# Two-layer MLA and S5 backbone: powers on VectorE, table loads tied to gates and units, other places for tables and gates

## The chip, the core and the metric

The kernel runs on one core of a Trainium2 chip. The metric is the device time of one execution in microseconds (us), as the median of several runs. PE is the matrix engine (TensorE), PEld its weight loads, DVE the vector engine, ACT the scalar engine, POOL is GpSimd, and SP the engine whose queue issues most DMAs. Each engine works through its own instructions in the order in which they stand in its queue, and so does each queue of DMA issues.

## The reference

The input is a latent stream of 512 tokens and a context of 256 tokens, 1024 wide. Layer 0 is multi-head latent attention with 16 heads and a SiLU gate, layer 1 a bidirectional S5 state-space layer with GLU. Both are modulated by a condition and end in a residual with LayerNorm. Cut to what matters here:

```python
# layer 0, attention over the low-rank keys (per head), then gate and projection
p = softmax((concat[q_pos @ keys_lat, q_free @ keys_ctx]) * scale)
o = p[:s] @ ckv_l + p[s:] @ ckv_c
y = ((o @ w_uv) * silu(gate)) @ w_out
x = layernorm(ALPHA * x + gt * y)
# layer 1, S5 in each direction, chunks of the sequence carried by a state
lam_bar = exp(lam * dt);  b_bar = ((lam_bar - 1) / lam) * bmat
powers  = exp(lam * dt * arange(1, S5_CHUNK + 1))
xs = scan(lam_bar, u @ b_bar) + powers * h;  y = real(xs @ cmat)
```

The S5 recurrence does not need the input to prepare its weights: powers of `lam_bar`, and from them tables that turn blocks of 8 tokens into states, states into outputs, and a short convolution kernel. The kernel makes these weights beside the work of layer 0 and leaves them in DRAM for layer 1.

## The kernel before

All tokens (768, latent and context) lie in the free dimension, channels in the 128 partitions. Products in fp32 are made of three matmuls of fp32r halves: `split` (L64) lets ACT copy the high half (`whi`) and DVE subtract it for the low half (`wlo`), and `mm3` (L80) issues hi by hi, hi by lo, lo by hi. `schedule_with_timeline_sim=True` (L1493) means that the framework puts the instructions of each engine in an order of its own, found with a simulated timeline; the order of the source is a priority, and a tile that is asked for takes a buffer as soon as its last user has released it.

Layer 0 runs through these stages.

- **Start** (L524 to L626). In four quarters `mod_part(q)` loads modulation weights into 24 staging tiles. They come in a cycle from pool `gv` (4 tiles `G`), pool `gm` (7 tiles `M`) and the two `pair` tiles. `h_make` makes the modulated input `hh`, `hl` (8 tiles of each). Meanwhile `s5_params` (L155) computes on DVE the step sizes, exponentials, cosines and the first power `lbr, lbi`, and then on POOL (`cmul`, six instructions of 128x128) the powers `pk` 0 to 7, their products with the coefficient in `cps`, the copies into `pw`, and four squarings `lt`, which go by five SP DMAs to `lamd`. Its tiles are the later `Qh0, Qh1, Ql0, Ql1, Vh, Vl, K1, K2, Ch, Cl` of attention: arena and `lt` lie in `Qh0, Qh1, Ql0`, `cps` in `K1, K2, Ch`.
- **Projections and gates** (L653 to L753). First come the four projections to `ckv`, `qd`, `kr`. Then `s5_coefs` (L295) turns `cps` with 16 PE transposes and stores it to `pind`; only after it do `K1, K2, Ch` come free for the keys. `gate(m)` for m = 0 to 15 (48 matmuls each) writes a gate tile. The first `KEPT = 4` stay in `G` tiles, the other twelve go through two `Gs` tiles to DRAM (`Gd`). Between the gates run 24 steps of the remaining modulation weights (`mod_more`, each a DMA of 768 or 512 KB into a `pair` tile), and `tables(n)`, which makes `S5IN = 20` of the `NCH = 32` chunks of state-out weights.
- **A chunk** (`s5_chunk`, L318): SP loads `cb`; POOL makes six products of 128x512 into `wo` and four smaller ones into `bk`; PE multiplies `bk` by `wo`; ACT and DVE take the result to `ks`; SP stores `wo` to `wod` and `ks` in eight DMAs to `kd`.
- **Attention** (L754 to L886): 16 heads of 5 units each, 80 units. Unit i takes `score(i + 2)`, transposes, values, `up_values` (multiplies by the gate, L840) and `softmax(i + 2)`. `prep(h + 1)` makes the next head's queries; in it the low halves `ul` (128x128, each head) and `wlo` (128x512, every second head) are subtracted on POOL (`split(..., pool)`, L460 and L500). `gate_back` reloads the twelve gates from DRAM. The other 12 chunks are made at the rate of 5 in 8 units. After unit `LAST = 19`, in two of three units, `win_early` makes the 32 pieces of state-in weights.
- **A piece of state-in weight** (`win_early`, L389): SP stores the piece made last (`wid`, L394), SP loads the next one's two tables of 512 KB (`pt` from `pind`, L375, into one of two `wo` tiles; `bt` from `Bc`, L376, into one of two halves of `btp`), and POOL makes the piece loaded before with six instructions of 128x512 (`win_make`, L378).
- **Out projection** (L889 to L998): 2 halves of 16 heads, 18 matmuls of 128x512 per head; ACT and DVE split `wraw` into `whi`, `wlo` in 7 buffers ahead. POOL has nothing to do here. Residual, norm and layer 1 follow; layer 1 reads `wid`, `wod`, `kd`, `lamd`.

## Time and profile before

| | us |
|---|---|
| median of 3 runs (1795.07 to 1800.5) | 1798.24 |
| the profiled execution | 1801.8 |
| its span, first to last instruction | 1800.0 |
| PE busy in the span | 1569.4 (87%) |
| DVE, ACT, POOL busy | 955.2, 731.0, 660.4 |
| mean granted clock of TensorE | 0.937 of full speed |

The page gives busy times for the whole span and for 40 equal slices. Busy PE is modelled, and at a lower granted clock the same matmul counts as busy for longer, so busy time is read together with the granted clock. The stages of layer 0 are read with a table of busy times in chosen stretches, the waits of each engine in such a stretch, and the instructions in order of time. A wait is put down to the instruction that came last.

### The profile page before, as it was taken

To read this page: it belongs to the slowest core of one execution; us is meant where nothing else is said; L and a number is where in the kernel's file an instruction comes from. 1 tells how busy PE (TensorE), PEld (TensorE's weight loads), DVE (VectorE), ACT (ScalarE), POOL (GpSimd) and SP (SyncE) were. 2 spreads that over 40 slices of the span, in tenths; PEclk is the share of its full clock that TensorE was granted. 3 is DMA by queue.
4 is the path that set the end of the run, shared out by engine and by line. 5 is a ranking of instruction groups with operands and counts; after the bars stand their busy time and mean duration, and the time that the engine had idled before them with its cause. 6 is when DMAs were issued, how large, how long until landed. Compare 5 with 4: busy or idle time off the path is not lost.

```text
span 1800.0 us, 26887 instructions
## 1 busy us (share of the span) xinstructions
PE 1569.4 (87%) x9870; PEld 1311.4 (73%) x9870; DVE 955.2 (53%) x2478; ACT 731.0 (41%) x1253; POOL 660.4 (37%) x705
## 2 busy tenths in 40 slices
PE   7547799988898789689999999889649999999997
PEld 4425568877787778678879999767437888888876
DVE  7252233476675567473472688868643333333336
ACT  2221122455564456272245666655444222222220
POOL 2999789899687777740000000000000000000022
PEclk9769899999998899889999999989769999999999
DMA  9226775532555555544327555599583333333342
GB/s 333 73 67 204 250 233 166 190 103 93 154 174 172 164 167 160 167 131 153 100 98 243 194 207 188 134 296 247 120 178 115 116 117 106 106 106 109 126 163 70
DMA packets 139340, 283.11 MB, mean 157 GB/s; under 512 B 38300, under 2 KB 70088, under 8 KB 139208
## 3 DMA queue, kind: packets, MB, share of 16 engines
q1 hardware_dynamic: 120904, 272.78, 49.5%
q10 hardware_dynamic: 18240, 8.59, 1.8%
q8 instruction: 78, 1.28, 0.3%
q14 instruction: 54, 0.44, 0.1%
q0 software_dynamic: 64, 0.03, 0.0%
HBM read 224.10 MB, written 56.97 MB: 156 GB/s over the span
## 4 chain that ended last, share of the span: by engine, by line
PE 49%; DMA 19%; POOL 17%; DVE 6%; issue 4%; ACT 3%; SPq 2%; ACTq 0%; POOLq 0%; DVEq 0%
PE mm L81 14%; PE mm L83 13%; PE mm L82 13%; DMA wo<-pind 5%; PE mm L1122 3%; DMA wid<-wo 3%; DMA toe<-kd 2%; DMA wraw<-in_wout_dram 1%; POOL wo L341 1%; POOL wo L338 1%; POOL wt L340 1%; POOL bk L352 1%; POOL wt L337 1%; DMA gd<-gg 1%; DMA pair<-in_w_mod_dram 1%
## 5 line engine op out<-in xcount | busy, mean ns | idle before, releaser
L65 DVE TENSOR_TENSOR wlo<-wraw,whi 128x1024 fp32r<-128x1024 f32 (+1 forms) x155 | 183.3, 1184 | 352.4 <-ACT whi L65 351.2
L1361 POOL TENSOR_TENSOR x<-x,row_g 128x1024 f32<-128x1024 f32 x4 | 11.4, 2852 | 968.1 <-DMA x<-x1d 968.1
L65 ACT CAST whi<-wraw 128x1024 fp32r<-128x1024 f32 (+1 forms) x155 | 149.5, 965 | 412.7 <-PE mm L82 278.2
L81 PE MATMUL mm<-st,whi 128*128 128x512 f32 x512 | 204.7, 400 | 7.4 <-ACT st L76 7.3
L83 PE MATMUL mm<-st,wlo 128*128 128x512 f32 x512 | 202.7, 396 | 0.0
L82 PE MATMUL mm<-st,whi 128*128 128x512 f32 x512 | 201.2, 393 | 0.5 <-DVE st L77 0.5
L81 PE MATMUL mm<-h,whi 128*128 128x512 f32 (+1 forms) x384 | 140.0, 365 | 12.3 <-DVE gg L1207 12.2
L82 PE MATMUL mm<-h,whi 128*128 128x512 f32 (+1 forms) x384 | 137.8, 359 | 0.8 <-DVE h L1067 0.8
L83 PE MATMUL mm<-h,wlo 128*128 128x512 f32 (+1 forms) x384 | 137.5, 359 | 0.0
L81 PEld LDWEIGHTS mm<-st,whi 128*128 128x128 f32 x512 | 97.5, 190 | 29.3 <-ACT st L76 8.7
L82 PEld LDWEIGHTS mm<-st,whi 128*128 128x128 f32 x512 | 97.3, 190 | 22.9 <-DVE st L77 1.5
L83 PEld LDWEIGHTS mm<-st,wlo 128*128 128x128 f32 x512 | 97.3, 190 | 22.6
L81 PE MATMUL mm<-hh,whi 128*128 128x512 f32 (+1 forms) x320 | 111.2, 358 | 2.9 <-DVE hh L589 2.9
L82 PE MATMUL mm<-hl,whi 128*128 128x512 f32 (+1 forms) x320 | 109.8, 346 | 0.0
L83 PE MATMUL mm<-hh,wlo 128*128 128x512 f32 (+1 forms) x320 | 108.7, 343 | 0.4 <-DVE wlo L65 0.3
L81 PEld LDWEIGHTS mm<-h,whi 128*128 128x128 f32 x384 | 73.6, 192 | 24.5 <-DVE gg L1207 13.3
L65 DVE TENSOR_TENSOR ptl<-tr,pth 128x384 fp32r<-128x384 f32 (+1 forms) x160 | 79.0, 523 | 17.1 <-ACT pth L65 16.3
L798 ACT ACTIVATE p<-sc,mx 128x768 f32<-128x768 f32 (+1 forms) x96 | 73.6, 767 | 32.2 <-DVE mx L797 32.0
L65 ACT CAST pth<-tr 128x384 fp32r<-128x384 f32 (+1 forms) x160 | 68.7, 462 | 41.9 <-PE tr L822 41.3
L797 DVE TENSOR_REDUCE mx<-sc 128x1 f32<-128x768 f32 (+1 forms) x96 | 73.6, 771 | 17.9 <-PE sc L787 16.7
L82 PEld LDWEIGHTS mm<-h,whi 128*128 128x128 f32 x384 | 73.7, 192 | 11.1 <-DVE h L1067 1.1
L83 PEld LDWEIGHTS mm<-h,wlo 128*128 128x128 f32 x384 | 73.5, 192 | 10.7
(371 smaller groups left out, 4188.3 us busy)
## 6 DMA issues: line engine op xcount, KB each, us to landing
wraw<-in_wglu_dram SPq DMA_DIRECT2D x64, 512.0 KB
wraw<-in_win_dram SPq DMA_DIRECT2D x52, 512.0 KB
wod<-wo SPq DMA_DIRECT2D x32, 512.0 KB
wo<-pind SPq DMA_DIRECT2D x32, 512.0 KB
pw<-in_Bc_dram SPq DMA_DIRECT2D x32, 512.0 KB
wid<-wo SPq DMA_DIRECT2D x32, 512.0 KB
pt<-wid SPq DMA_DIRECT2D x32, 512.0 KB
wo<-wod SPq DMA_DIRECT2D x32, 512.0 KB
```

What stands on the lines that cost most here:

```text
L65: return act.copy(hi, src).ins, (eng or dve).tensor_tensor(lo, src, f(hi), op=ALU.subtract).ins
L81: pe.matmul(ps, lh, rh, start=first, stop=False)
L82: pe.matmul(ps, lh, rl, start=False, stop=False)
L83: pe.matmul(ps, ll, rh, start=False, stop=last)
L337: pool.tensor_tensor(t2, ci, pi, op=ALU.mult)
L338: pool.tensor_tensor(wr, t1, t2, op=ALU.subtract)
L340: pool.tensor_tensor(t2, ci, pr, op=ALU.mult)
L341: pool.tensor_tensor(wi, t1, t2, op=ALU.add)
L352: pool.tensor_tensor(bk[rows, :, :, 16 * d:16 * d + 16], b1[rows], b2[rows], op=ALU.add)
L797: dve.reduce_max(mx[:, 1:2], s, axis=AX.X, negate=True)
L798: act.activation(p[:, a:b], s, AF.Exp, bias=mx[:, 1:2], scale=1.0, accum_out=mx[:, 2:3])
L1122: pe.matmul(o[:, r, 96 * q:96 * (q + 1)], wi[:, q, r, :], us[m][:, 4 * (c % 2) + q, :], start=True, stop=True)
```

## The change

1. **Powers on VectorE.** The chain of powers `pk` (8 `cmul`), the squarings `lt` (4), the first product `clr, cli` and five negations run on DVE. POOL keeps the eight products `cps` and the copies into `pw`. All eight `pk` have places of their own (`K1, K2, Ch`), `cps` lies in three `G` tiles. `s5_params` is a generator that is taken up again in the quarters of the start. The five stores to `lamd` are issued by ACT.
2. **Last gates kept.** Gates 12 to 15 stay in `G`, gates 0 to 11 go to DRAM and back (the first `AHEAD = 3` are asked for before attention, then one per head). `s5_coefs` runs after gate 1. The staging tiles of the start are the 16 tiles of `hh`, `hl`, then 7 `M` and one `pair`, so each of the 24 loads has its own.
3. **Table loads tied.** Before a load of `cb` (three buffers now) DVE copies one column of the gate just made, or of a softmax tile `p` of the next unit, into it; the load waits for that copy. The same is done for `bt`.
4. **`ul` and the rope `wlo` on DVE**, by the default of `split`.
5. **17 chunks** in the gates instead of 20; the other 15 in attention at 4 in 7 units, up to unit 26.
6. **State-in weights.** `pt` goes through three places: a tile `ext` that holds `cci` and the two `bk` before, and the two `wo`. They are made in 5 of 8 units after unit 26, and 24 of 32 there. The last eight are made in the out projection (`win_c`), in a pool of three `pt`, three `bt`, with their DMAs issued by ACT; the pool `w` of layer 1's weights opens after it closes.

```diff
-    KEPT = 4
+    KEPT, AHEAD = 4, 3
-    GR, NCH, S5IN = 128, 32, 20
+    GR, NCH, S5IN, WIN = 128, 32, 17, 24
...
-        cmul(clr, cli, cr, ci, lbr, lbi, t1, t2)
-        cps = [slots(6) for _ in range(3)]
+        cmul(clr, cli, cr, ci, lbr, lbi, t1, t2, dve)
+        u1, u2 = T1[:, 1, :], T1[:, 2, :]
+        cps, pk = [[slots(6, t) for _ in range(3)] for t in (take2, take)]
...
         for k in range(8):
+            p, q = pk[k], lt[0] if k == 7 else pk[k + 1]
+            cmul(q[:, 0, :], q[:, 1, :], p[:, 0, :], p[:, 1, :], lbr, lbi, t1, t2, dve)
+            cmul(cps[k][:, 0, :], cps[k][:, 1, :], p[:, 0, :], p[:, 1, :], clr, cli, u1, u2)
             pool.tensor_copy(pw[0:64, :, k, :], p[0:64])
             pool.tensor_copy(pw[64:128, :, 7 - k, :], p[64:128])
-            cmul(cps[k][:, 0, :], cps[k][:, 1, :], p[:, 0, :], p[:, 1, :], clr, cli, t1, t2)
-            q = lt[0] if k == 7 else pk[(k + 1) % 3]
-            cmul(q[:, 0, :], q[:, 1, :], p[:, 0, :], p[:, 1, :], lbr, lbi, t1, t2)
-            p = q
+            if k % 3 == 2:
+                yield cps
...
-            sp.dma_start(out=lamd[:, l], in_=lt[l])
+            act.dma_start(out=lamd[:, l], in_=lt[l])
...
         def load(c):
-            cbs[c] = work.tile([P, 4, 2, 32], F32, name="cb", bufs=2)
+            cbs[c] = work.tile([P, 4, 2, 32], F32, name="cb", bufs=3)
+            dve.tensor_copy(cbs[c][:, 0, 0, 0:1], after)
             sp.dma_start(out=cbs[c], in_=I["CB"][:, 4 * c:4 * c + 4])
...
-                split(*st["w"], raw, pool)
+                split(*st["w"], raw)
...
-                split(*st["u"], wa[:, 384:512], pool)
+                split(*st["u"], wa[:, 384:512])
...
-            wtile = itertools.cycle(["G"] * KEPT + ["M"] * 7 + ["pair"] * 2)
+            wtile = iter(["hh", "hl"] * KC + ["M"] * 7 + ["pair"])
...
-            s5_coefs(cps, mm, t512)
...
-                G.append(gv.tile([P, T], F32, name="G") if m < KEPT else gsp.tile([P, T], F32, name="Gs"))
+                G.append(gv.tile([P, T], F32, name="G") if m >= HEADS - KEPT else gsp.tile([P, T], F32, name="Gs"))
...
-                tables(3 if m == 0 else 1 + (m in (5, 10)))
+                if m == 1:
+                    s5_coefs(cps, mm, t512)
+                tables(1 + (m == 0), m)
...
-            LAST = 8 * (NCH - S5IN) // 5
+            LAST = 7 * (NCH - S5IN) // 4
...
-                    gate_back(h + KEPT)
+                    gate_back(h + AHEAD)
...
-                if LAST < i < len(units) - 1 and i % 3 != 0:
-                    win_early(lambda: (work.tile([P, 4, 2, P], F32, name="wo", bufs=2), btp[:, len(early) % 2]),
+                    pts = itertools.cycle([(s5c, "ext", [P, 9 * GR], 1)] + [(work, "wo", [P, 4, 2, P], 2)] * 2)
+                if i > LAST and 5 * i // 8 > 5 * (i - 1) // 8:
+                    def tabs():
+                        where, name, shape, bufs = next(pts)
+                        pt = where.tile(shape, F32, name=name, bufs=bufs)
...
+                        bt = btp[:, len(early) % 2]
+                        dve.tensor_copy(bt[:, 0, 0, 0:1], un[i + 1]["p"][:, 0:1])
+                        return pt, bt
+                    win_early(tabs, lambda: [work.tile([P, 4, P], F32, name=f"wt{k}", bufs=1) for k in (1, 2)],
+                              len(early) > NCH - WIN)
...
+    def win_c(more=True):
+        win_early(lambda: [wcp.tile([P, 4, 2, P], F32, name=n, bufs=3) for n in ("pt", "bt")],
+                  lambda: [wcp.tile([P, 4, P], F32, name=f"t{i}") for i in range(2)], more, act)
...
         if h == 7:
             gvs.close()
+            wces, (wcp,) = pools(dict(name="winc", bufs=2, side="right"))
         for tt in range(NT):
             out_mm(o[tt], tt, h, 0)
+        if h >= 7:
+            win_c()
...
-    assert not (early or loaded or stores)
+    while early or loaded or stores:
+        win_c()
+    wces.close()
```

## Rows read from the trace of the kernel before

**Rows 1.** The page's slices of 45 us: busy tenths of PE and POOL.

```profile
PE   7547799988898789689999999889649999999997
POOL 2999789899687777740000000000000000000022
```

**Rows 2.** Busy us (instructions) by stretch: PE, PEld, DVE, ACT, POOL; clock, DMA share, GB/s.

```profile
55.00:73.00 18.00, 17.33 (x90) 14.52 (x89) 6.73 (x7) 8.31 (x16) 16.69 (x29) 0.92 0.32 98
73.00:116.00 43.00, 13.92 (x43) 8.72 (x44) 13.02 (x14) 9.73 (x23) 40.14 (x70) 0.60 0.19 52
116.00:204.00 88.00, 57.36 (x487) 39.62 (x489) 33.66 (x49) 15.69 (x28) 84.01 (x102) 0.81 0.58 188
204.00:273.00 69.00, 64.16 (x606) 49.23 (x599) 21.27 (x34) 15.87 (x33) 52.47 (x59) 0.95 0.74 243
...
340.00:455.00 115.00, 104.95 (x1010) 90.76 (x1009) 76.93 (x162) 65.98 (x159) 108.38 (x126) 0.99 0.38 128
455.00:797.00 342.00, 282.22 (x1819) 253.13 (x1818) 216.83 (x444) 184.38 (x434) 256.84 (x208) 0.91 0.57 165
```

**Rows 3.** What PE waited for, 0 to 330 us: total us, times, longest.

```profile
PE modps L103 <- DMA pair<-in_w_mod_dram: 24.6, 8, 6.9
PE mm L300 <- POOL Ch L238: 12.9, 2, 6.8
PE mm L300 <- POOL K L238: 11.8, 3, 6.2
```

**Rows 4.** POOL in order of time: start us, us, line.

```profile
38.54 1.39 POOL L238 TENSOR_TENSOR Vh<-Ql,Vh 128x128 f32<-128x128 f32 x1
...
79.22 0.74 POOL L281 COPY pw<-Ql 64x256 f32<-64x256 f32 x1
...
81.66 0.45 POOL L238 TENSOR_TENSOR K<-Ql,Vh 128x128 f32<-128x128 f32 x1
...
86.60 0.39 POOL L281 COPY pw<-Vh 64x256 f32<-64x256 f32 x1
```

**Rows 5.** DVE in order of time, start and gates, to the first softmax reduction.

```profile
37.05 0.28 DVE L264 TENSOR_TENSOR Vl<-Qh,Vh 128x128 f32<-128x128 f32 x1
...
38.40 1.22 DVE L65 TENSOR_TENSOR wlo<-wraw,whi 128x1024 fp32r<-128x1024 f32 x1
...
116.52 0.69 DVE L689 SCALAR_TENSOR_TENSOR G<-G,mm 128x512 f32<-128x512 f32 x1 [0.50 <-ACT G L688]
...
204.19 0.69 DVE L689 SCALAR_TENSOR_TENSOR Gs<-Gs,mm 128x512 f32<-128x512 f32 x1 [8.66 <-ACT Gs L688]
...
273.07 0.69 DVE L689 SCALAR_TENSOR_TENSOR Gs<-Gs,mm 128x512 f32<-128x512 f32 x1
...
340.70 0.96 DVE L797 TENSOR_REDUCE mx<-sc 128x1 f32<-128x768 f32 x1 [2.12 <-PE sc L787]
```

**Rows 6.** What PE waited for, 460 to 800 us.

```profile
PE mm L83 <- POOL ul L65: 37.4, 5, 9.8
PE tr L822 <- DVE ptl L65: 12.6, 2, 12.4
```

**Rows 7.** What the SP queue waited for, 455 to 790 us.

```profile
SPq L394 <- POOL wo L385: 153.0, 31, 7.8
SPq L375 <- DMA wid<-wo: 79.3, 30, 6.1
```

**Rows 8.** DVE's products with the gate, two heads apart, and the last one.

```profile
589.73 0.41 DVE L840 TENSOR_TENSOR G<-mm,G 128x256 f32<-128x256 f32 x1
...
647.65 0.42 DVE L840 TENSOR_TENSOR G<-mm,G 128x256 f32<-128x256 f32 x1
...
794.77 0.42 DVE L840 TENSOR_TENSOR G<-mm,G 128x256 f32<-128x256 f32 x1 [0.38 <-PE mm L83]
```

**Rows 9.** A table load on the chain that ended last: start us, us.

```profile
585.84 8.22 DMA wo<-pind
```

**Rows 10.** ACT in the out projection, in order of time.

```profile
851.28 0.62 ACT L65 CAST whi<-wraw 128x512 fp32r<-128x512 f32 x1 [3.46 <-PE mm L83]
```

67 lines of the change are left out of this document (36 added, 31 removed).

## Prediction, made before the changed kernel was run

> **What bounds the kernel now.** The page's slices come first: PE is near full only from the ninth slice on, and dips again from the twelfth to the nineteenth, and just there POOL is at 7 to 9 tenths; after the eighteenth slice POOL is idle and PE full [rows 1]. So layer 0 is where PE loses time, and POOL is the suspect. The table of stretches makes that a list [rows 2]. From 73 to 116 us PE works 13.9 of 43 us at a granted clock of 0.60 while POOL works 40.1; from 116 to 204 it is 57.4 of 88 at 0.81, POOL 84.0. From 455 to 797 it is 282 of 342 at 0.91, POOL 257. A busy POOL proves nothing, so the third view is what PE waited for. At the start it is the transposes of `cps` (L300, 24.7 us in 5 waits) and the modulation weights (24.6 us in 8) [rows 3]. In attention it is `ul`, 37.4 us in 5 waits [rows 6]: a subtraction of half a microsecond that stands in POOL's queue behind six long products which themselves wait for a table. What these products wait for is seen from SP: the load of `pt` waits 79.3 us in 30 times for the store of the piece before, since that store frees its buffer [rows 7]. From 797 us on the change touches only the out projection.
>
> I make the sum from three marks: the first gate's product at 116.5 us, the first softmax reduction at 340.7 us [rows 5], and attention's last product with the gate at 794.8 us [rows 8].
>
> **Powers, coefficients and first gates.** A round of the chain on POOL took 7.38 us, from one copy into `pw` to the next (79.22 to 86.60), for 12 products and 2 copies, so 0.53 us each [rows 4]. Eight rounds with 6 products and 2 copies are 8 x 8 x 0.53 = 34 us; DVE has the coefficients at 37 us [rows 5], so POOL ends the rounds near 74 us and the chunks can follow; the squarings are gone from its queue (24 products, 13 us, beside the 8 x 6 powers, 25 us). DVE gains 54 + 24 products of 0.28 us [rows 5], at most 22 us, and 7 smaller ones. They run beside the loads of the start and between 55 and 73 us, where DVE works 6.7 of 18 us [rows 2]; if that cover fails they delay the last `hh`, 0 to 5 us, and I take 0. ACT's five stores cost it about 2 us in the same stretch (busy 8.3 of 18). The transposes of `cps` no longer stand ahead of `rms` and the first gate. With the 24.7 us of waits gone, and `K1` free near 74 us, the first gate's product comes at about 90 us instead of 116.5: 26.5 us earlier. Bounds are 84 (POOL free earlier than PE) and 100 (the keys still wait for `pw` copies).
>
> The trace shows POOL slowed beside DVE: a 128x128 product took 1.39 us at 38.5 us, where DVE began a 1.22 us subtraction at 38.4, and 0.45 us at 81.7 [rows 4, 5]. The Trainium skill (SBUF — State Buffer, "SBUF: two separate sides") says that DVE with two SBUF inputs and GpSimd exclude each other from a shared port pair for a whole instruction. By it the 78 moved products could push POOL's rounds out by up to 22 us, an estimate, to 96 us; by the row alone they end at 74. The first chunk's table waits for gate 0 anyway, so the sum would change by some 5 us.
>
> **Gates.** From gate 4's product to gate 9's there are 68.9 us [rows 5], 13.8 us per gate, with three modulation loads in each and the DMA at 0.74 share [rows 2]. From gate 9's to the first softmax are 67.6 us [rows 5]. After, POOL has 17 chunks instead of 20; at 84 us of 88 it was the pace from 116 to 204, at 52.5 of 69 it no longer was. So I take 13.8 us for each of gates 0 to 8: 90 + 9 x 13.8 + 67.6 = 282 us, against 340.7: **59 us less**. The low bound is 11.5 us per gate (between 13.8 and the 10 us of gates 9 to 15), which with the rest gives 84 + 104 + 67.6 = 256 and a gain of 85; the high bound is 16 us (four gates more are stored in the stretch where DMA is busiest), 100 + 144 + 67.6 = 312, a gain of 29. The tied table loads add a wait: DVE's copy into `cb` waits until POOL is through with the chunk three before, and behind it on DVE stand the gate's product (L689) and the weights' low halves, for which PE waits; on SP the load waits for the copy, and behind it stand the next gate's weights, the modulation loads and the stores of `Gs`. A chunk takes POOL less than 10 us and a gate 10 to 14, so I cost it at nothing; without that cover it is the difference per gate. The 12 gates stored and reloaded are as many as before, and the staging tiles change nothing as long as the start is bound by the loads themselves.
>
> **Attention.** Three paces follow each other. Up to unit 26 there are 15 chunks. In 340 to 455 us POOL was busy 108.4 us [rows 2] with 12 of them and 5 us of `ul` and `wlo`: 8.6 us each, 9.2 with gaps, so 138 us (the `ul` and `wlo`, now on DVE, cost it 0.3 to 0.7 us per head where it works 217 of 342 us; hidden). Then 24 pieces of state-in weights. POOL's 256.8 us in 455 to 797 hold 32 pieces and 11 us of `ul` and `wlo`: 7.7 us each. Before, each took the 342 - 10 us of the stretch over 32, 10.4 us, that is 7.7 plus the 2.6 us that SP waited for the store (79.3 over 30) [rows 7]. A third place takes that store out of the loop. A load takes 8.2 us [rows 9], about the time of a piece, so I take 7.7 + 0.6 = 8.3 us, 200 us for 24. Last come 15 units without POOL. Two heads took 57.9 us [rows 8] with about 8.6 us of waiting for `ul` (the mean of the five waits is 7.5, the largest 9.8 [rows 6]) and, by the clock of 0.91, some 2.5 us of half speed: 47 us for ten units, 4.7 each, 71 us. With 5 us for the last two units' lag: 138 + 200 + 71 + 5 = 414 us against 454: **40 us less**. `ul`'s 37.4 us and the 12.6 us at the end (a weight load behind the last pieces on SP [rows 6]) are inside it, not added. PE's own pace would give 80 x 4.7 + 5 = 381, 73 us less; the loop of 10.4 us kept gives 138 + 250 + 71 + 5 = 464, 10 us more. Here the new wait is DVE's copy into `bt`: it waits for POOL's piece two before, and behind it stand the reductions, the low halves of `p` and the products with the gate, so PE.
>
> **Out projection.** Eight pieces of 7.7 us, 62 us of POOL that had nothing to do there. ACT now stands still where a store waits for POOL, up to 7.7 us, with `whi` casts and the six copies of the half's end behind it. ACT was waiting for PE to free a buffer (3.46 us each time [rows 10]), seven tiles ahead, so casts are hidden; a copy that is caught costs PE directly. I take 2 us, bounds 0 and 10. Layer 1's weights load later, but before their use.
>
> **Sum.** 1801.8 - 59 - 40 + 2 = 1704.8 us for a profiled execution. The median before is 3.6 us below the profiled one, so I say 1701 us.
>
> **Rivals.**
> (a) POOL slips off the path altogether: gains of 80 and 73 us, out projection at 0, 1798 - 153 = 1645 us. For it speaks that PE needs POOL in attention only for a chunk's 16 small matmuls; against it that DVE's copies tie PE to POOL again, two pieces back.
> (b) The ties keep the old paces: 16 us per gate with the first at 92 us, 304 us and 37 us less; pieces at 10.4 us, 10 us more; out projection 8 us more: 1798 - 19 = 1779 us. SP's queue, where all these loads stand in one line, speaks for it.
> (c) Slower: the copy into `bt`, the load and the piece run one after the other because the copy comes behind the piece that POOL is working on. Then a piece costs 7.7 + 8.2 us, 16 us with handovers, 24 are 384 us instead of 200, and attention takes 598 us; with the other terms 1701 + 184 = 1885 us. It decides from about 12.3 us per piece, where the gains of 97 us are used up. Against it: there are two `bt` halves, and the load for one can run beside the piece of the other.
> (d) The change does not do what it says: the framework's order puts the chain of powers on DVE so late, or the transposes again so early, that the first gate stays at 116 us, and pieces keep their 10.4 us. Then only the chunks fewer and the tail move, 1785 to 1800 us.
>
> **How the numbers follow.** The forecast has a chance of 0.52, (a) 0.17, (b) 0.17, (c) 0.08, (d) 0.06. The forecast's own range is 1665 to 1740. Eight in ten have to take in (b) and nearly (a): 1648 to 1782 us. A measurement of this kernel tells about 0.3% (5.4 us) from no change; that band belongs to (d) mainly, so same has 0.04, slower 0.08, faster 0.88.
>
> **What would show it.** After: no wait of L300 for POOL's products, gate 0's product near 90 us, the first softmax reduction near 280; in attention no wait of PE for `ul`, pieces 8 to 9 us apart on POOL, attention some 414 us; POOL busy some 60 us in the out projection with PE still full. The prediction is wrong if DVE is seen idle before its copies into `cb` or `bt` until POOL ends (b, c), if PE waits for modulation weights for more than the 24.6 us of before, or if ACT's copies at the half's end stand behind a store.

## The result, and the profile after

The changed kernel took 1826.1 us in the median, the kernel before 1799.4 us in the same session: a ratio of 1.0138, with an interval of 1.0112 to 1.0164. The profiled execution of the changed kernel took 1826.06 us, with a span of 1823.9 us. The forecast was 1701 us. It was wrong, in sign too. One execution below that was kept as a trace, that of no_bt_tie, took over 1.5% longer than the fastest of its kernel; it is left out of that run's median and ratio, and its stretches are not compared.

All line numbers of this part are those of the changed kernel, where the product with the gate is L695, the first softmax reduction L807, attention's product with the gate L850, the copy into `cb` L324 and the one into `bt` L901. (Where an edit adds or removes a line, the numbers of its run are off by one or two.)

The marks come first: VectorE in order of time, as in [rows 5, 8].

```profile
99.20 0.68 DVE L695 SCALAR_TENSOR_TENSOR Gs<-Gs,mm 128x512 f32<-128x512 f32 x1
...
260.98 0.69 DVE L695 SCALAR_TENSOR_TENSOR Gs<-Gs,mm 128x512 f32<-128x512 f32 x1
...
334.19 0.96 DVE L807 TENSOR_REDUCE mx<-sc 128x1 f32<-128x768 f32 x1 [2.12 <-PE sc L797]
...
786.29 0.42 DVE L850 TENSOR_TENSOR G<-mm,G 128x256 f32<-128x256 f32 x1 [0.38 <-PE mm L83]
```

They split the change in the profiled spans, 1823.9 - 1800.0 = +23.9 us, into three terms:

| stretch | before | after | change | forecast |
|---|---|---|---|---|
| start to first softmax | 340.7 | 334.2 | -6.5 | -59 |
| first softmax to last product with the gate | 454.1 | 452.1 | -2.0 | -40 |
| from there to the end | 1005.2 | 1037.6 | +32.4 | +2 |

So two gains stayed out and a loss came where almost none was expected. The table of stretches answers [rows 2]: busy us with instruction counts in brackets for PE, PEld, DVE, ACT and POOL, then the granted clock, the DMA share and GB/s. The last two lines are the first 90 us of the output projection.

```profile
99.00:204.00 105.00, 77.23 (x621) 55.06 (x625) 41.00 (x68) 24.66 (x52) 68.46 (x70) 0.87 0.66 208
204.00:261.00 57.00, 47.81 (x397) 37.45 (x387) 14.46 (x30) 10.63 (x22) 35.45 (x40) 0.88 0.64 206
334.00:455.00 121.00, 101.33 (x904) 87.90 (x902) 76.27 (x170) 63.51 (x153) 94.94 (x110) 0.95 0.32 110
455.00:786.00 331.00, 284.89 (x2004) 251.00 (x2005) 230.53 (x495) 184.29 (x438) 221.73 (x184) 0.96 0.46 142
786.00:846.00 60.00, 56.43 (x243) 44.84 (x242) 25.80 (x31) 19.18 (x29) 22.20 (x18) 1.00 0.50 143
846.00:876.00 30.00, 10.88 (x47) 8.67 (x46) 6.96 (x9) 5.96 (x11) 19.58 (x15) 0.73 0.67 184
```

The last line is the most striking: PE works 10.9 of 30 us. In the same place before (855 to 885 us) it worked all 30:

```profile
855.00:885.00 30.00, 30.00 (x131) 24.42 (x130) 15.56 (x25) 8.13 (x14) 0.00 (x0) 1.00 0.43 132
```

In the stretches above, POOL is no longer the busy engine: it had 84.0 of 88 us in 116 to 204 before [rows 2], now 68.5 of 105. It waits.

**Gates.** What POOL waited for between 60 and 345 us (us in total, times, longest), and POOL's first chunk in order of time:

```profile
POOL wt L339 <- DMA cb<-in_CB_dram: 86.1, 12, 23.8
```

```profile
103.64 1.10 POOL L339 TENSOR_TENSOR wt<-cb,pw 128x512 f32<-128x512 f32 x1 [23.77 <-DMA cb<-in_CB_dram]
```

POOL had done its last product for the coefficients at 79.9 us and stood until 103.6, since the table load is tied to gate 0. Over the gates it stood 86.1 us for such tables.

**Attention.** DVE, then PE, in order of time around 540 us (`bt` lies in a tile that is named `pw`):

```profile
532.71 0.56 DVE L65 TENSOR_TENSOR ptl<-tr,pth 128x384 fp32r<-128x384 f32 x1
548.34 0.15 DVE L901 COPY pw<-p 128x1 f32<-128x1 f32 x1 [15.07 <-POOL wo L388]
548.41 0.55 DVE L65 TENSOR_TENSOR ptl<-tr,pth 128x384 fp32r<-128x384 f32 x1
```

```profile
536.07 0.49 PE L832 MATMUL tr<-ident,p 128*128 128x128 f32 x3
549.01 0.90 PE L832 MATMUL tr<-ident,p 128*128 128x128 f32 x3 [12.45 <-DVE ptl L65]
```

This is the tie at work. The copy writes one column of the `bt` half that POOL is still reading, so DVE stands 15.07 us until POOL's last instruction (L388) on that piece. The low half `ptl` behind it in DVE's queue comes late, and PE stands 12.45 us for it. The wait that PE had for `ul` (37.4 us [rows 6]) is gone, and this one and its like are in its place.

**Output projection.** A stretch of the chain that ended last (start us, us, what), and ACT in order of time:

```profile
799.57 3.36 DMA wraw<-in_wout_dram
...
836.76 7.16 DMA wraw<-in_wout_dram
...
847.86 9.21 DMA wraw<-in_wout_dram
```

```profile
869.98 0.62 ACT L65 CAST whi<-wraw 128x512 fp32r<-128x512 f32 x1 [2.92 <-DMA wraw<-in_wout_dram]
870.06 0.32 ACTq L397 DMA_DIRECT2D wid<-pt  x1
870.41 0.61 ACTq L379 DMA_DIRECT2D bt<-in_Bc_dram  x1
...
873.76 0.62 ACT L65 CAST whi<-wraw 128x512 fp32r<-128x512 f32 x1 [3.16 <-POOL t L384]
874.28 2.04 ACT L994 COPY acc<-mm 128x512 f32<-128x512 f32 x4
```

A 256 KB tile of output weights took 3.4 us at 799.6 us, before ACT issued the first load of a late piece (803.1 us); beside these loads it takes 7 to 9 us, and two are under way at most. ACT's six copies of the finished accumulators stand in its queue behind the casts of those tiles and behind the pieces' issues; they come 88.0 us after the last product with the gate, 61.3 us before the change. PE waits 19.1 us for them, and the granted clock of the stretch is 0.73.

```profile
PE mm L81 <- ACT acc L994: 19.1, 1, 19.1
```

How much of the +32.4 us belongs to the projection itself shows the last mean and variance of the norm at its end, before and after the change:

```profile
932.30 0.20 DVE L906 BATCH_NORM_AGGREGATE bnmv<-bnst 128x2 f32<-128x12 f32 x1
```

```profile
958.11 0.20 DVE L924 BATCH_NORM_AGGREGATE bnmv<-bnst 128x2 f32<-128x12 f32 x1
```

It comes 137.5 us after the last product with the gate before the change and 171.8 us after it, 34.3 us later. From there to the end it is 867.7 and 865.8 us. So the loss lies in the projection, and the new order of layer 1's loads, which could have been behind it, shows none. Below, this mark is called "the norm".

### The profile page after: what moved, and what is told of

Its sections match the earlier page's. It is cut to its first block, busy times and chain, and to the rows that moved or that the text cites. A ratio compares the mean times of both kernels' runs of the same rounds, so it can differ in the third digit from the quotient of the medians.

```text
span 1823.9 us, 27020 instructions
## 1 busy us (share of the span) xinstructions
PE 1585.2 (87%) x9870; PEld 1318.2 (72%) x9870; DVE 1006.3 (55%) x2643; ACT 729.9 (40%) x1253; POOL 606.5 (33%) x596
## 4 chain that ended last, share of the span: by engine, by line
PE 38%; DMA 15%; DVE 8%; POOL 4%; ACT 4%; issue 2%; SPq 0%; ACTq 0%; POOLq 0%; DVEq 0%
PE mm L81 11%; PE mm L82 11%; PE mm L83 11%; DMA wraw<-in_wout_dram 4%; PE mm L1148 3%; DMA pw<-in_Bc_dram 2%; DMA toe<-kd 2%; DVE wlo L65 2%; DMA wo<-wod 1%; DMA wraw<-in_win_dram 1%; ACT whi L65 1%; DMA gd<-gg 1%; DMA bt<-in_Bc_dram 1%; PE mm L1284 1%; POOL wt L384 1%
## 5 line engine op out<-in xcount | busy, mean ns | idle before, releaser
L81 PE MATMUL mm<-h,whi 128*128 128x512 f32 (+1 forms) x384 | 141.0, 368 | 11.9 <-DVE gg L1233 11.7
L83 PE MATMUL mm<-hh,wlo 128*128 128x512 f32 (+1 forms) x320 | 113.1, 358 | 3.5 <-DVE wlo L65 3.5
L82 PE MATMUL mm<-hl,whi 128*128 128x512 f32 (+1 forms) x320 | 114.6, 360 | 0.0
L81 PE MATMUL mm<-whi,vh 128*128 128x512 f32 x186 | 72.0, 408 | 25.6 <-ACT acc L994 19.1
L832 PE MATMUL tr<-ident,p 128*128 128x128 f32 x448 | 68.1, 276 | 23.2 <-DVE ptl L65 23.1
```

What stands on the lines that cost most here:

```text
L81: pe.matmul(ps, lh, rh, start=first, stop=False)
L82: pe.matmul(ps, lh, rl, start=False, stop=False)
L83: pe.matmul(ps, ll, rh, start=False, stop=last)
L832: pe.transpose(tp[:, n, :], p[:, j * P:(j + 1) * P], ident)
```

## The experiments

| run | edit, against the changed kernel | median us | ratio to before, interval |
|---|---|---|---|
| the change | | 1826.1 | 1.0138 (1.0112 to 1.0164) |
| all_in_attention | all 32 pieces in attention | 1830.5 | 1.0159 (1.0133 to 1.0185) |
| win_on_sp | late pieces' transfers on SP | 1824.2 | 1.0122 (1.0073 to 1.0171) |
| wraw4 | four places for output weights | 1819.1 | 1.0095 (1.0064 to 1.0126) |
| powers_pool | powers on POOL again | 1826.2 | 1.0139 (1.0097 to 1.0181) |
| no_gate_ties | no ties in the gates | 1815.2 | 1.0068 (1.0038 to 1.0098) |
| no_bt_tie | no ties for `bt` | 1802.6 | 1.0012 (0.9983 to 1.0041) |
| no_unit_ties | no ties in attention | 1774.4 | 0.9847 (0.9824 to 0.9870) |
| no_ties | no ties at all | 1767.9 | 0.9809 (0.9782 to 0.9836) |
| untied_late | no_unit_ties, pieces later in the source | 1768.7 | 0.9822 (0.9783 to 0.9862) |
| untied_28 | no_unit_ties, 28 pieces in attention | 1769.3 | 0.9813 (0.9782 to 0.9843) |
| untied_28_late | untied_late and untied_28 together | 1781.0 | 0.9869 (0.9821 to 0.9918) |
| chunks12 | no_unit_ties, 12 chunks in the gates | 1794.6 | 0.9955 (0.9927 to 0.9982) |
| nt_after | no_ties, pieces behind the copies | 1777.7 | 0.9879 (0.9857 to 0.9902) |
| nt_pool | no_ties, pieces' transfers on POOL | 1771.7 | 0.9836 (0.9785 to 0.9886) |
| nt_pool28 | nt_pool_wraw4, 28 pieces in attention | 1768.1 | 0.9811 (0.9763 to 0.9859) |
| nt_sp_wraw4 | no_ties, SP, four places | 1764.7 | 0.9803 (0.9744 to 0.9861) |
| nt_pool_wraw4 | no_ties, POOL, four places | 1757.2 | 0.9741 (0.9691 to 0.9791) |
| splits_only | the kernel before, with `ul` and `wlo` on DVE | 1815.5 | 1.0069 (1.0049 to 1.0089) |

The kernel before took 1799.4 to 1803.2 us beside these runs, so runs are compared by their ratios. Stretches are read from one profiled execution per run. The runs show how far such a reading can be trusted: attention with no ties in it and 24 pieces was 400.0, 400.1, 400.7, 403.6, 405.7, 407.5 and 408.4 us in seven of them, and the stretch after it, with the change's own output projection, 1030.9 to 1043.4 us in six (the change, powers_pool, no_gate_ties, no_unit_ties, no_ties, chunks12). A difference under 8 us in the first or under 13 us in the second means nothing here. Most of the latter's scatter lies behind the norm (860 to 871 us over all runs); up to the norm the same six took 169.2 to 174.7 us.

### The ties

```diff
 # no_unit_ties: attention; no_gate_ties: the same in the gates; no_ties: both
-                    chunk(work, mm, n_s5 - 1, NCH - 1, un[i + 1]["p"][:, 0:1])
+                    chunk(work, mm, n_s5 - 1, NCH - 1, None)
...
-                        dve.tensor_copy(bt[:, 0, 0, 0:1], un[i + 1]["p"][:, 0:1])
```

> The changed kernel without DVE's one-column copies into cb and bt in attention; the loads follow when their buffers are free. Theory: those copies hold DVE behind POOL (32.8 + 6.1 us for bt's places, 9.5 for cb), and with it reductions and low halves for PE, which waits 23.1 us for the transposes' input: attention from the first softmax to the last product with the gate falls from 452 to 415-440 us and the whole by 12-37 us. Rival: POOL itself is the pace of the pieces (SP waits 89.8 us for the store that frees a place, POOL 31.5 for bt): DVE no longer waits for POOL, but PE waits for something else, and attention stays at 447-457 us, the whole at 1820-1832.

Measured: 1774.4 us, 52 less than the change; attention 408.4 us. The theory held, and by more than it had given. Its rival fell: POOL's pieces did not hold attention at its old pace. What PE waited for in attention, first of the changed kernel, then without the ties (us, times, longest):

```profile
PE tr L832 <- DVE ptl L65: 23.1, 9, 12.4
```

```profile
PE mm L509 <- DMA wmod<-in_absw_dram: 8.9, 3, 3.6
...
PE tr L833 <- DVE ptl L65: 1.0, 3, 0.5
```

The wait for `ptl` falls from 23.1 to 1.0 us. The rest of the 44 us by which attention got shorter is not one wait of PE: the first chunk of attention began at 352.8 us where it began at 334 without the ties, and PE's mean clock in the whole execution went from 0.942 to 0.947.

```profile
352.82 1.23 POOL L339 TENSOR_TENSOR wt<-cb,pw 128x512 f32<-128x512 f32 x1 [20.77 <-DVE mx L809]
```

Here POOL stands 20.8 us for a table whose load was tied to a unit that PE had not reached. To tell the two kinds of tie apart:

> The changed kernel without the copy into bt that holds back a piece's second table; the copies into cb stay, in attention too. Without both kinds attention took 408.4 us instead of 452.1 and the whole 1774 instead of 1826. Theory A (the bt copies do it: DVE stood behind POOL 32.8 + 6.1 us for them, with the reductions and low halves behind): attention 410-420 us, the whole 1776-1790. Theory B (the cb copies do it: they stop the first chunk of attention for 20.8 us and the chunks at 447-467 us, so the pieces start at 518 us instead of 495): attention 425-440, the whole 1795-1815. If both halves of the loss are alike, 425-435 us.

Measured: 1802.6 us, inside theory B's range for the whole. By the ratios (1.0138 with both kinds, 1.0012, 0.9847 with neither) the `bt` copies carry some 23 us and the `cb` copies some 30. With intervals of 0.2 to 0.3% either way the two aren't told apart, and no run took the `cb` copies away alone. So a load that is held back costs in two ways: the engine that holds it stands (15.07 us before `bt`), and the consumer's work starts late (the first piece at 518 us with both kinds, at 495 without).

> The changed kernel without DVE's one-column copy that holds a chunk's table load back until its gate is there; everything else is kept. Theory: the ties starve POOL (86.1 us of waits for cb, 23.8 the longest, between 60 and 345 us), and PE's small matmuls of a chunk wait for POOL some 30 us in all. Without them POOL starts the chunks at 80 us, the waits for cb fall under 30 us, the first softmax comes at 300-320 us instead of 334.2, and the whole falls by 14-34 us to 1792-1812. Rival: the gates are paced by the loads of the modulation weights (PE waits 15.8 us for pairs) and by the DMA engines; then POOL is earlier but the first softmax stays at 330-336 and the whole at 1820-1830. A second rival: loads of tables that run ahead push the modulation loads back, first softmax 340 or later, 1832 us or more.

Measured: 1815.2 us, first softmax at 326.1 us. POOL's first chunk came at 57 us, but gate 0 moved back from 99.2 to 108.5 and gate 9 came forward only from 261.0 to 257.4. The theory had the sign, but its least gain was 14 us and 11 came; its rival (330 to 336 us for the softmax) fell too. Over the runs with 17 chunks the first softmax came at 329.7 to 335.1 us with these ties (nine) and at 325.0 to 330.8 without (seven), 5 us apart in the mean. So in the gates the ties cost some 5 to 11 us, not the 86.1 us that POOL stood.

> The changed kernel without any copy that ties a table load, in the gates or in attention. The two edits alone gave 1815.2 and 1774.4 us, against 1826.1. Theory (they act in different stretches and add): 11 us less than without the unit ties alone, 1758-1768 us, first softmax at 322-328, attention 404-412. Rival (the earlier chunks only give POOL an earlier start that attention doesn't need): first softmax 322-328 but attention 412-420, the whole 1768-1778.

Measured: 1767.9 us; first softmax at 325.0, attention 400.7, and 1038.4 us from there to the end. The two edits add, as the theory had it.

### The start and the gates

```diff
 # powers_pool: the products of the chain on POOL again (two more such lines: clr, cli and lt)
-            cmul(q[:, 0, :], q[:, 1, :], p[:, 0, :], p[:, 1, :], lbr, lbi, t1, t2, dve)
+            cmul(q[:, 0, :], q[:, 1, :], p[:, 0, :], p[:, 1, :], lbr, lbi, t1, t2)
```

> The changed kernel with the powers, the squarings and the first product of the coefficients on POOL again, in the new places and the new order; the ties stay. Theory (the products of DVE cost 0.50-0.55 us beside POOL's and hold the h tiles: the last cast of h at 61-69 us, before 54-57; DVE is through at 80 us): with them on POOL the start is 5-10 us shorter on DVE, but POOL ends its rounds at about 100-110 us instead of 79; as the first table comes at 103.6 us anyway, the first gate's product moves by -8 to +3 us from 99.2, the first softmax stays within 326-340 us, the whole within 1815-1832. Rival (POOL's early end is what brought gate 0 forward from 116.5): gate 0 back at 110-117, first softmax 345-352, the whole 1836-1845.

Measured: 1826.2 us, no change. Gate 0, gate 9 and the first softmax of this run, on DVE:

```profile
86.48 0.67 DVE L695 SCALAR_TENSOR_TENSOR Gs<-Gs,mm 128x512 f32<-128x512 f32 x1
...
258.04 0.69 DVE L695 SCALAR_TENSOR_TENSOR Gs<-Gs,mm 128x512 f32<-128x512 f32 x1
...
332.41 0.96 DVE L807 TENSOR_REDUCE mx<-sc 128x1 f32<-128x768 f32 x1 [3.54 <-PE sc L797]
```

Gate 0 came 12.7 us earlier than in the change, more than was expected, and 3 us of it were left at gate 9. The rival fell: POOL ended its last product for the coefficients at 109.7 us here, so it was not POOL's early end, for which the powers had gone to DVE, that brought gate 0 forward from 116.5 us. On DVE they held the start back: the last `hl` ended at 69.1 us in the change, at 59.8 in this run, at 57.6 before. Over four kernels gate 0 came at 86.5, 99.2, 108.2 and 108.5 us, and gate 9 at 258.0, 261.0, 253.9 and 257.4. Gate 0 doesn't set gate 9.

What does set it was tried with fewer chunks:

```diff
-    GR, NCH, S5IN, WIN = 128, 32, 17, 24
+    GR, NCH, S5IN, WIN = 128, 32, 12, 24
```

> The changed kernel without the unit ties, with 12 chunks instead of 17 in the gate stage and 20 in attention. Theory 1 (the chunks pace the gates, by POOL and by PE's wait for it): the first softmax comes 25-45 us before 333.8, at 289-309. Theory 2 (the modulation loads and their DMA share of 0.8 pace gates 1 to 9, PE's own work the rest): the first gates stay at 18 us, and the first softmax gains only what PE no longer computes, five chunks of some 2 us: 318-330. In attention the five chunks of 9.1 us come back: the whole 1770-1800 us.

Measured: 1794.6 us, first softmax at 322.0. The edit turned out to say little: it takes its five chunks from behind gate 9 (the first twelve run at the old times, 103 to 264 us), and gate 9 came at 259.7 us. Behind gate 9 five chunks fewer gave 11 us, some 2 us each, as theory 2 had it for PE's share in them. In attention the chunks cost more than they had saved, 435 us instead of 408. What paces gates 0 to 9 stays open. The rows show that they moved the same bytes: 88 x 188 + 69 x 243 = 33.3 MB in 157 us before [rows 2], 105 x 208 + 57 x 206 = 33.6 MB in 162 us after, and PE stood idle 35 and 37 us in them. That could speak for the modulation loads, whose number is the same in both; but without ties 225 x 146 = 32.9 MB passed in 146 us (108 to 254 us), so it is no fixed rate, and no run here took any load away.

### The split alone

```diff
 # the kernel before
-                split(*st["u"], wa[:, 384:512], pool)
+                split(*st["u"], wa[:, 384:512])
```

> The kernel before with one part of the change alone: ul and the low half of the rotary weights on DVE instead of POOL. PE waited 37.4 us in 5 times for ul. Theory: those waits go, PE is then held by what POOL makes 10.4 us a piece, which it needs only through the places of the pieces; attention falls from 454 to 415-435 us and the whole by 20-40 us, to 1762-1782 us. Rival 1: the pieces at 10.4 us are themselves the pace through the program's order, so attention stays at 447-456 us and the whole within 5 us of before. Rival 2: DVE, now with 0.5 us more per head ahead of its reductions, loses what PE gains: 1800-1808 us.

Measured: 1815.5 us, slower than before by 0.5 to 0.9%; attention 468.1 us. None of the three had this. PE's waits in attention, and SP's:

```profile
PE mm L504 <- DMA wmod<-in_absw_dram: 49.7, 6, 12.7
```

```profile
SPq L375 <- DMA wid<-wo: 76.9, 30, 5.8
```

The wait for `ul` is gone and a wait for the next thing has come: the head's weights `absw`, whose load stands on SP among the table loads and stores of the pieces, and SP still waits 76.9 us for the stores (79.3 before [rows 7]). With the third place and no ties, PE waited 8.9 us for the same load. That points to the third place as what made room, though no run has it alone; the split alone only uncovered SP's queue.

### The output projection

Its loss has three suspects: ACT's queue, the transfers themselves, and the number of late pieces.

```diff
 # all_in_attention
-    GR, NCH, S5IN, WIN = 128, 32, 17, 24
+    GR, NCH, S5IN, WIN = 128, 32, 17, 32
 # wraw4
-        raw = owp.tile([P, 512], F32, name="wraw", bufs=2)
+        raw = owp.tile([P, 512], F32, name="wraw", bufs=4)
 # win_on_sp (the runs with POOL's queue have pool there)
-                  lambda: [wcp.tile([P, 4, P], F32, name=f"t{i}") for i in range(2)], more, act)
+                  lambda: [wcp.tile([P, 4, P], F32, name=f"t{i}") for i in range(2)], more, sp)
```

> The changed kernel with all 32 pieces of the state-in weights started in attention and none in the out projection (24 -> 32, one number). Theory 1: the eight late pieces cost the out projection about 32 us (last product with the gate to the end 1037.6 us, before 1005.2), because their loads and stores stand in ACT's queue ahead of the casts and copies and beside the loads of the output weights. Then that stretch falls back to 1003-1010 us, the 19.1 us that PE waits for ACT's copy of an accumulator is gone, and attention grows by at most 8 pieces of 8-10 us less the cover it has, 10-40 us: the whole between 1795 and 1835 us. Theory 2 (the out projection lost its time to the new order of layer 1's loads and not to the pieces): the stretch stays near 1037 us, and the whole is 1835-1865 us.

Measured: 1830.5 us, attention 459.4, and 1034.9 us after it. The whole lies in theory 1's range and the stretch in theory 2's; the trace decides. The loss moved, it didn't go: the copies' wait is gone, and PE stands at the seam to the projection instead (the norm at 172.2 us, as in the change).

```profile
PE mm L81 <- ACT vh L76: 31.0, 1, 31.0
```

ACT's halves of the values stand behind casts that wait up to 10.0 us each for output weights, and those loads are on SP among the last pieces' loads and stores.

> The changed kernel with the loads and stores of the late pieces issued by SP instead of ACT; POOL's work and the bytes are the same. Theory 1a: the loss comes from ACT's queue, where an issue that waits for POOL holds casts and copies: the 1037.6 us from the last product with the gate to the end fall to 1005-1015, the whole to 1793-1806 us. Theory 1b: the loss comes from the transfers, which share the DMA engines with the output weights (PE busy 25.9 of 45 us in 855-900, ACT waiting 74.1 us in 19 times for a weight tile): the stretch stays at 1030-1045, and with SP's own loads of weights now behind waits for POOL it may grow to 1060; the whole 1820-1850 us.

> The changed kernel with four places instead of two for the raw tiles of the output weights, so that four loads of 256 KB can be under way; nothing else is changed. ACT waits 74.1 us in 19 times for such a tile and PE 19.1 us for the accumulator copies that stand behind the casts. Theory 1 (each load comes later because it shares the engines with the pieces' 512 KB, and two places can't cover that): with four places the last product with the gate to the end falls from 1037.6 to 1008-1020 us and the whole to 1796-1809 us. Theory 2 (the DMA engines have no more to give in that stretch): 1030-1040 us and 1818-1830.

Measured: 1824.2 and 1819.1 us, 1032.3 and 1031.7 us after attention: each little, as theories 1b and 2 had it (the norm at 172.5 and 165.0 us, 171.8 in the change). But what ACT waited for says why. In the first 90 us after attention, for the kernel before, for the change, with four places, and (without ties) with POOL's queue and four places:

```profile
ACT whi L65 <- DMA wraw<-in_wout_dram: 19.9, 11, 2.7
```

```profile
ACT whi L65 <- DMA wraw<-in_wout_dram: 60.1, 14, 8.2
```

```profile
ACT whi L65 <- DMA wraw<-in_wout_dram: 24.0, 7, 8.3
ACT whi L65 <- issue: 20.8, 3, 12.6
ACT whi L65 <- DMA wid<-pt: 18.0, 3, 10.1
```

```profile
ACT whi L65 <- DMA wraw<-in_wout_dram: 27.7, 10, 7.1
ACT whi L65 <- PE mm L83: 26.4, 8, 5.4
```

With four places the wait for tiles falls from 60.1 to 24.0 us, and 38.8 us of standing at ACT's own issues appear, which wait for a piece's store. With those issues on POOL too, half of ACT's waiting is for PE again, as before the change.

> The changed kernel without any tie, the late pieces' loads and stores issued by POOL, with the change's two places for the raw output weights. With four places as well: 1757.2 us, 1024.2 us from the last product with the gate to the end, copies 67.7 us after it. Theory 1 (it is the issues standing on ACT): the same within 5 us, the stretch 1020-1030, the whole 1752-1763, without the 4.1 us that PE stood at the seam for memory. Theory 2 (it is the two places, which can't cover a load beside the pieces' transfers): copies at 80-90 us, the stretch 1033-1040, the whole 1763-1772.

> As the run with POOL's queue, but with the pieces' transfers on SP, in one line with the weight loads. Theory 1 (queues that stand still): the weight loads stand behind issues that wait for POOL, at most four tiles deep, so half of the loss or more stays, 1750-1768 us. Theory 2 (shortage of the DMA engines): the same as with POOL's queue within 5 us.

> The changed kernel without any tie, the late pieces' loads and stores issued by POOL, which waits for them anyway, and four places for the raw output weights. No issue of a piece stands on ACT or SP any more. Theory 1 (the loss is queues that stand still: on ACT casts and copies behind an issue, on SP the weight loads): PE no longer waits for the copies (22.1 us), the stretch falls from 1038.4 to 1008-1018 us, the whole to 1738-1750. Theory 2 (the DMA engines are short in that stretch): copies stay at 80-90 us, the whole at 1760-1772.

Measured: POOL's queue with two places took 1771.7 us (1037.4 after attention, ACT 64.6 us at the tiles); SP's with four 1764.7 us (1043.3); POOL's with four 1757.2 us (1024.2, copies 67.7 us after the last product). Up to the norm these are 170.0, 173.2 and 157.8 us, with 170.4 for no_ties. So POOL's queue alone did nothing, four places alone 7 us (above), both together 13 us. In the medians that is just visible (0.9741 against 0.9809 for no_ties, with intervals that touch). For POOL's queue alone theory 2 held; for the two together theory 1 by half: some 20 us stay (157.8 against 137.5). Its second stretch, 60 to 90 us after the last product, with the DMA share the last but one number:

```profile
794.00:824.00 30.00, 30.00 (x132) 24.52 (x131) 24.61 (x21) 7.06 (x12) 22.31 (x20) 1.00 0.89 221
```

PE works all 30 us here, where it worked 10.9 of 30 in the change, with the DMA engines at 0.89. SP's and POOL's medians are 7 us apart with intervals that overlap, and SP's profile is its longest execution; but up to the norm its 173.2 us are those of the change, and PE waits 17.2 us for the copies there, for none with POOL's queue.

Of the 20 us that stay, the trace shows where about half go: 3.7 us at the seam, for ACT's halves of the values, and the following, on ACT, DVE and PE.

```profile
861.97 2.00 ACT L65 CAST whi<-wraw 128x1024 fp32r<-128x1024 f32 x2 [15.01 <-DMA wid<-pt]
```

```profile
863.05 2.36 DVE L65 TENSOR_TENSOR wlo<-wraw,whi 128x1024 fp32r<-128x1024 f32 x2 [12.82 <-ACT whi L65]
```

```profile
873.36 1.09 PE L1087 MATMUL mm<-ident,acc 128*128 128x128 f32 x4 [9.49 <-DVE acc L1070]
```

ACT's cast of layer 1's first weights stands 15.0 us for the store of a late piece, DVE's low halves stand behind that cast, the norm's products behind those, and PE waits 9.5 us for them (2.1 in no_ties). The rest isn't traced to a wait. DVE works 24.6 of 30 us in the stretch above, since its own instructions became longer: its subtraction of a 128x512 low half took 0.69 us in the mean before the change (795 to 885 us), and 1.69 us beside POOL's pieces here (764 to 854 us).

```profile
L65 DVE TENSOR_TENSOR wlo<-wraw,whi 128x512 fp32r<-128x512 f32 x27 | 18.4, 688 | 36.4 <-ACT whi L65 36.4
```

```profile
L65 DVE TENSOR_TENSOR wlo<-wraw,whi 128x512 fp32r<-128x512 f32 x21 | 34.9, 1689 | 29.3 <-ACT whi L65 29.3
```

PE waited only 1.7 us for low halves, so this isn't shown to cost much; it is a load on DVE that work on an idle POOL brought along.

> The changed kernel without the copies that tie table loads to units in attention, and with the eight late pieces moved from the second part of the output projection's first half (heads 7 to 15) to its second half, one piece per head. Against the same kernel with the pieces where the change has them: 1774.4 us, 1030.8 us from the last product with the gate to the end, accumulator copies 87 us after that product (61 us before the change). Theory 1 (the loss lies in the transfers beside the output weights: ACT waits 66.7 us in 20 times for a weight tile there and 74.1 in the changed kernel, PE 21.5 and 19.1 for the copies behind): the copies come at 61-65 us again and the stretch takes 1005-1012 us, the whole 1749-1757. Theory 2 (the pieces cost the same wherever the out projection has them, because PE has no more cover in its second half): copies at 61-65 us, but the stretch stays at 1025-1035, the whole 1768-1780.

> The changed kernel without any tie (1767.9 us, 1038.4 us from the last product with the gate to the end, accumulator copies 87.8 us after that product), with the late pieces ordered behind the last accumulator copy on ACT, so that they really run in the second half. Theory 1 (what stands ahead of the copies costs PE, and the second half has cover): copies at 61-65 us, the stretch 1008-1018, the whole 1738-1750. Theory 2 (the second half pays the same, or layer 1's weights, whose memory the pieces hold until then, come late): copies at 61-65 us, the stretch 1025-1045, the whole 1755-1775.

```diff
 # untied_late, nt_after: win_c() goes from the first loop over heads to the second
-        if h >= 7:
-            win_c()
...
 # nt_after, in the second loop; copied is the last accumulator copy
+        with tc.issue_after(copied):
+            win_c()
```

Measured: 1768.7 us for the move in the source, 1777.7 us for the order. The first changed nothing: the pieces started at 760 to 841 us as without it (772 to 848), because the order of issue on ACT doesn't follow the source there. It tells nothing about the place. With the order, the copies came at 62.1 us as before the change, and the stretch took 1043.0 us all the same (the norm at 172.0): theory 2, with a whole 3 us above its range. ACT stood at its issues in the second half:

```profile
ACT whi L65 <- issue: 21.2, 1, 21.2
ACT bnmv L138 <- DVE bnmv L925: 17.3, 3, 12.7
```

```profile
PE mm L81 <- DVE bnmv L925: 15.8, 1, 15.8
```

```diff
 # untied_28 and nt_pool28; the second edit in nt_pool28 alone
-    GR, NCH, S5IN, WIN = 128, 32, 17, 24
+    GR, NCH, S5IN, WIN = 128, 32, 17, 28
...
-                    sp.dma_start(out=raw, in_=I["wout0"][0, :, 0:512])
+                    act.dma_start(out=raw, in_=I["wout0"][0, :, 0:512])
```

> The changed kernel without the unit ties, with 28 pieces in attention and four in the out projection (24 and 8 in the change). Without the ties POOL is through with its 24 pieces at 702 us, 40 us before attention's last product with the gate, so four more of 8.3 us fit: attention stays at 406-414 us. Theory 1 (loss per late piece): four late pieces instead of eight give back about half of the 26 us, the stretch after attention takes 1012-1022 us, the whole 1756-1768. Theory 2 (the pieces near the end of attention hold the memory that the out projection's first tiles take, as with all 32 in attention, where PE stood 31 us for it): PE waits at the seam, and the whole stays at 1768-1785.

> The changed kernel without the unit ties, 28 pieces in attention, the last four in the second half of the out projection. If each of the two moves takes its part of the same 26 us, this has nothing over the pieces moved alone: 1747-1757 us, the stretch after attention 1003-1010. If the pieces cost PE by their number wherever they are, four give back half: 1758-1768. If the pieces at the end of attention hold the seam, 1770-1785.

> The run with POOL's queue and four places, with 28 pieces in attention instead of 24 and the projection's first weight tile loaded through ACT's queue instead of SP's (where it stood behind the pieces' loads and stores: PE waited 11.4 us for it with 28 pieces, ACT 12.2). Theory 1 (the loss goes by the number of late pieces): half of the remaining 20 us of the stretch, and attention within 5 us of 407.5: the whole 1743-1752. Theory 2 (the pieces at the end of attention hold PE anyway, by memory or by the weights of the heads on SP): attention 415-425, what the stretch gains is lost before it, the whole 1755-1768.

Measured: 1769.3, 1781.0 and 1768.1 us. By the whole that is theory 2 of the first and of the last, and the third case of the second. With ACT issuing, four late pieces instead of eight gave back half of the loss, as theory 1 of the first said (the norm at 152.9 and 153.7 us, 169.5 in no_unit_ties), and attention took it (421.6 and 425.4 us): PE stood 11.4 us for `pair`, which ACT made late, because ACT stood 12.2 us for the projection's first weight tile behind the pieces on SP. With POOL's queue and four places, four pieces gave nothing (158.3 against 157.8; PE stood 10.2 us for the copies again), and attention took 414.5 us, with 11.9 us of waits for `absw` and 5.2 for `pair`. So in these runs the loss went by the number of late pieces only where ACT issued them.

The fastest version is nt_pool_wraw4: the change without its ties, with POOL issuing what it waits for, and four places, 1757.2 us, 0.9741 of the kernel before.

## Why the prediction was wrong

Of the three signs of being wrong that the prediction named, two came: DVE idle before a copy into `bt` until POOL ends, and ACT's copies late at the half's end. PE's wait for modulation weights did not grow (15.8 us between gates 0 and 9, 24.6 before).

**The first reading.** [rows 1] were misread: PE is at nine tenths from the sixth to the eighth slice already, and after POOL has gone idle it falls to six and four tenths in the 29th and 30th, in layer 1. Layer 0 is not the only place where PE loses time; no term of the sum hangs on that.

**The start: direction right, by luck, and worth nothing.** The first gate came at 99.2 us, forecast 90 with a bound of 100. L300's wait for POOL is gone. But the powers on DVE had no part in it: with them on POOL again, and POOL late, gate 0 came at 86.5 us. What brought it forward is in the rest of the edit, and which part isn't shown. DVE's products were taken at 0.28 us [rows 5] from a moment in which POOL had hardly begun. Beside POOL they took 0.48 us in the mean of 63 products (median 0.51); the 15 that had POOL idle took 0.28. One of each, the idle one first:

```profile
46.59 0.29 DVE L241 TENSOR_TENSOR K<-Ql,Vh 128x128 f32<-128x128 f32 x1
...
61.22 0.55 DVE L241 TENSOR_TENSOR Qh<-Ql,Vh 128x128 f32<-128x128 f32 x1
```

That made 78 products some 34 us of DVE (63 x 0.48 + 15 x 0.28) instead of 22, and the cover that I named (the last `hh`, at 0 to 5 us) gave way: DVE worked 17.75 of 18 us between 55 and 73 us. POOL ended its rounds at 79.9 us, forecast 74. The prediction's sentence on the Trainium skill (SBUF — State Buffer, "SBUF: two separate sides") had POOL pushed out by up to 22 us by the shared port. The trace agrees that the two engines hinder each other, with DVE's product near twice as long beside POOL; but POOL was late by 6 us only, and stood 5.5 us of that time for DVE's powers.

**The gates: the step that failed is the chain "90 + 9 x 13.8 + 67.6".** It took the pace of gates 4 to 9 of the kernel before for all nine and began it at gate 0. Gates 0 to 9 took 161.8 us, 18.0 each, where the chain had 124.2; before, they took 156.6 us [rows 5]. Of the 52.4 us by which the chain was short (281.8 against 334.2), 37.6 are here, 9.2 at gate 0, and 5.6 from gate 9 to the softmax. The runs show that gate 9 comes at 254 to 261 us whether gate 0 comes at 86 or at 108, so a gain at gate 0 is no gain. A rate read in one part of a stretch was carried to a part with another limit, and which limit that is stays open. The tie in the gates, put at nothing, cost 5 to 11 us. Rival (b) had 16 us per gate.

**Attention: the tie was not counted, and the rest came right by cancellation.** Without ties attention took 400 to 408 us, forecast 414, but not in the forecast's parts. In no_unit_ties the chunks took 137 us (forecast 138), then POOL stood 23.5 us for the first piece's table (no term), the 24 pieces took 207 us (200), and the rest 40 us (76):

```profile
494.53 1.29 POOL L384 TENSOR_TENSOR wt<-ext,pw 128x512 f32<-128x512 f32 x1 [23.54 <-DMA ext<-pind]
```

So that the sum is near is luck. (The last part also took 2.5 us off two heads for the clock of 0.91, where 9% of their 57.9 us are 5.2; that is 4 us of the 36.) With the ties attention took 452. The prediction named the new wait and what stands behind it on DVE, and rival (c) gave its mechanism; but the forecast's sum had no term for it, and (c) had it at every piece (16 us), where it came at a few: 15.07 us at one copy, 9.8 at another, 20.8 us of POOL at the first chunk. The term was 44 us, and it ate the whole gain.

**`ul`:** I held its 37.4 us to be inside the sum, and not added. That was right: the split alone lost 0.7%, and a wait for `absw` came in its place.

**The output projection: the term of 2 us, bounds 0 to 10, was 32 us.** The term that failed is the price of the late pieces. The prediction priced POOL's products (idle engine) and ACT's standing at a store, and named the copies of the half's end as what PE would feel. It priced no transfer: eight pieces bring 8 x 3 x 512 KB = 12 MB into a stretch where 256 KB tiles for PE must arrive every 4 us through two places. That ACT was seven tiles ahead [rows 10] was a cover against one late issue, not against a lower rate: ACT's wait at the tiles in those 90 us grew from 19.9 to 60.1 us. The Trainium skill (DMA: Bandwidth & Descriptors, "Issuing engines are not separate DMA queues") says that transfers issued by the scalar, sync or gpsimd engine run on the same 16 DMA engines and interleave. The runs agree as far as the queue alone goes: ACT's, SP's and POOL's gave 1037.6, 1032.3 and 1037.4 us with two places (the norm at 171.8, 172.5 and 170.0). They add that the issuing engine's other work stands behind an issue that waits.

**Sum.** The measured terms are -6.5 - 2.0 + 32.4 = +23.9 us against the forecast's -59 - 40 + 2. Without ties they are -15.7 - 53.4 + 33.2 = -35.9, which is the span of no_ties (1764.1 us).

**What stays open:** what paces gates 0 to 9, what brought gate 0 forward, and half of the 20 us that stay in the output projection with POOL's queue and four places.

## What to carry to other kernels

A one-column write that times a load puts the buffer's last reader into the queue of the engine that writes it: before adding one, name the instruction that frees the buffer and everything behind the write. When a wait goes, look for what stands next in the same queue; the split of `ul` alone changed PE's wait for one instruction into a wait for another load on SP. And work that is moved to an idle engine brings its transfers along: price their bytes, their places and the queue that issues them in the stretch they go to, not the products alone. A forecast whose sum comes out is not confirmed until its parts are: attention's parts missed by 23 us one way and 36 the other.

## What had not been expected of the hardware

A 128x128 fp32 product of two SBUF operands on VectorE took 0.28 us with POOL idle and 0.48 us beside POOL's products (means of 15 and 63 instructions of one execution). A 128x512 subtraction took 0.69 us in the mean with POOL idle, 1.06 us beside the pieces when ACT issued their transfers (no_ties) and 1.82 us when POOL did (nt_pool); why the issuing engine matters isn't shown. A 256 KB weight load took 7.2 to 9.2 us beside the 512 KB transfers of the pieces, with a DMA share of only 0.50 to 0.67 in that stretch. And an earlier first gate, by 22 us between runs, left the tenth gate where it was.
